# A Hymba-style layer on one core: GLA norm weights moved into W_out's rows, half a column group of FF1 weights loaded early, squares written elsewhere

## The chip, the cores and the metric

The kernel runs on one core of a Trainium2 chip (trn2). The metric is the device time of one execution in microseconds (us). Engines are named as the profile names them: PE (TensorE, matmuls; PEld is its weight load), DVE (VectorE), ACT (ScalarE), POOL (GpSimd) and SP (SyncE, which issues most DMAs). L12 is line 12 of the kernel before.

## The reference

One decoder layer with two parallel mixers, on 2048 tokens of width 1024, all in float32. The part that the change touches, shortened:

```python
nx = rmsnorm(h, attn_norm_g)
proj = einsum('bsd,dp->bsp', nx, w_in)
gq, gk, gv, gr, glow, dq, dk_, dv_ = split(proj)
o_a = gla_mixer(gq, gk, gv, glog)                       # 4 heads, gated linear attention
o_a = o_a * lax.rsqrt(mean(o_a * o_a, axis=-1) + EPS)
o_a = o_a * gla_norm_g.reshape(GLA_HEADS, GLA_DV)        # 512 norm weights
o_a = o_a.reshape(B, S, 512) * silu(gr)
o_b = dilated_mixer(dq, dk_, dv_, rel_bias)              # 8 heads, three windows
h = h + concat([o_a, o_b]) @ w_out
y = rmsnorm(h, mlp_norm_g)
h = h + square(relu(y @ w_ff1)) @ w_ff2                  # 1024 -> 4096 -> 1024
out = rmsnorm(h, final_norm_g)
```

The norm weights multiply the 512 columns of the first mixer, whose product with W_out's first 512 rows follows, so they can stand at three places: in the gate values silu(gr), in o_a, or in W_out's rows.

## The kernel before, in words

**Number format.** Each float32 operand is split in two, a rounded high part (ACT, `AF.Copy`) and the rest (DVE, source minus high part): `split`, L489 to L491. A product is three matmuls, high by high, rest by high, high by rest (L140 to L142). The large products are done blockwise with 7 instead of 8 block products ("jobs" j = 1 to 7), whose operands are sums of blocks.

**Stages**, one behind the other with some overlap: the input projections (to about 520 us, in two passes of 1024 tokens each), attention of both mixers (to about 870 us), W_out with the second norm (850 to 1045 us), FF1 (to 1750 us) and FF2. In the projections the order of each engine is the program's; behind them a scheduler sets each engine's order from its own estimate of times, and buffers are slots of a common pool, so a load starts when the last reader of its slot is done.

**Gate values.** For the column group "gr" the projection's result goes through silu in `acc` (L353 ACT exponential, L354 DVE product), L355 multiplies it on POOL by the norm weights, held in all partitions as `gnB` in the tile `misc`, and SP stores it to `srD`. The same stage keeps DVE busy with weight sums and splits (`wcomb`, L288 to L300) and with the blocks' sums (`acc`, L342, L442 to L458). SP's queue is in order, so its weight loads (`wraw`) and the stores of q (`qD`) stand in line with these stores.

**W_out.** `load_wo` (L1115) loads 8 row chunks of 128; the chunks c < 4 belong to the first mixer and are split into the blocks (1, c) and (12, c), the others are kept whole. `sum_wo` (L1130) loads chunks c and c + 4 together, forms four differences on POOL and stores them to `wtD`, from where `mix_wo` (L1143) loads and splits them later. All of this runs within attention's time.

**The second norm.** `norm_row` (L1289) takes one row block of 128 tokens: the squares with their sum on ACT (L1292, written to `scr`, which nobody reads), the scaling on DVE (L1294), eight transposes on PE, two copies on ACT into the block's half of `bb` (L1300, quarters `hb4`), and stores to `hTD`. `norm_sums` (L1303) forms four sums of a pair of blocks on DVE (L1307 to L1310) and stores them too. `bb` holds one pair; `gs` holds the norm weights of the second norm in its first half, and `scr` is its second half.

**FF1.** 16 column groups of 256 (g), each in two halves k of four row chunks. `load_w1` (L1381) brings a half by a POOL DMA into one of two raw tiles `w1raw`, `prep1` (L1389) splits and sums for a job. W_out's loop calls the first loads: group 0 at its step 49, group 1 at step 54, and prepares FF1's jobs from step 54. The first jobs are mixed of both groups: (0,1), (0,2), (0,6), (1,1), (0,5), (1,2), and so on, pairs of group and job; (1,1) needs half 0 of group 1, (1,2) needs half 1.

## Time and profile before

| | |
|---|---|
| three runs | 2235.83, 2241.91, 2242.97 us; median 2241.91 us |
| the profiled execution | 2242.91 us, its span 2241.1 us, mean granted clock 0.997 |
| POOL's multiplies L355 | 32, in 79 to 131 us and in 329 to 381 us |
| POOL's loads of FF1's raw weights L1387 | 64 of 512 KB, from 1025.4 to 1617.0 us |
| ACT's squares L1292 | 16, from 879.2 to 1063.5 us |

How to read the profile: a line of groups gives the source line, engine, operation, output tile <- input tiles, shape, count, then busy time and mean duration of one, and the idle time of the engine ahead of them with what ended it. A line of waits gives who waited for whom, the total in us, how often, and the longest. A line of the timeline gives start, duration, engine, line, operation; in brackets the idle time before it and its releaser. A line of windows gives the stretch, then for each engine busy time and count, then TensorE's granted clock (1.00 is full), the DMA engines' share and GB/s. Instructions overlap a little in the timeline, so the chain of waits shows the same ones somewhat shorter.

### The profile page before, as it was taken

How to read it: one execution, taken by the hardware profiler on the slowest of the kernel's cores; microseconds unless marked ns; L12 is line 12 of the kernel's file. 1: busy time of each engine (PE TensorE's matmuls, PEld its weight loads, DVE VectorE, ACT ScalarE, POOL GpSimd, SP SyncE). 2: the span in 40 equal slices, each digit the busy share in tenths (PEclk: the TensorE clock that was granted, in tenths of full speed). 3: DMA queues.
4: the chain of work that ended last, by engine and by line, in shares of the span. 5: the costliest groups of instructions: out<-in, count | busy, mean ns of one | idle time of the engine just before them, and what ended most of it. 6: DMA issues, size and time to landing. Idle time of an engine off the chain costs nothing.

```text
span 2241.1 us, 35330 instructions
## 1 busy us (share of the span) xinstructions
PE 2212.8 (99%) x12420; PEld 1918.8 (86%) x12420; DVE 1680.8 (75%) x3173; ACT 1253.5 (56%) x2506; POOL 533.6 (24%) x535
## 2 busy tenths in 40 slices
PE   9999999999999999999999999999999999999998
PEld 8978998799999998887888888888888888888877
DVE  8787868666677677778777788777685697576798
ACT  7675446435787785555655566555555433333446
POOL 1110001016577673000000000000006222031462
PEclk9999999999999999999999999999999999999999
DMA  6467854787977877767744456555489988677775
GB/s 214 141 188 229 256 165 121 213 250 251 312 256 222 271 214 241 247 225 249 220 141 149 140 177 199 165 167 167 130 279 287 306 282 276 216 250 253 250 258 197
DMA packets 340934, 491.79 MB, mean 219 GB/s; under 512 B 20503, under 2 KB 237162, under 8 KB 330004
## 3 DMA queue, kind: packets, MB, share of 16 engines
q1 hardware_dynamic: 319842, 394.88, 54.6%
q0 software_dynamic: 13568, 41.95, 7.6%
q10 hardware_dynamic: 7346, 52.70, 6.3%
q8 instruction: 98, 1.61, 0.3%
q14 instruction: 80, 0.66, 0.1%
HBM read 335.52 MB, written 158.66 MB: 221 GB/s over the span
## 4 chain that ended last, share of the span: by engine, by line
PE 68%; issue 16%; DVE 7%; DMA 5%; POOL 2%; ACT 1%; SPq 0%; POOLq 0%; ACTq 0%; DVEq 0%
PE ps_a L141 7%; PE ps_a L142 6%; PE ps_a L140 6%; PE ps_c L141 5%; PE ps_c L142 5%; PE ps_c L140 5%; PE ps_a L909 4%; PE ps_d L141 3%; PE ps_d L142 3%; PE ps_d L140 3%; PE ps_o L141 3%; PE ps_o L140 3%; PE ps_o L142 3%; PE ps_d L890 3%; PE ps_c L872 2%
## 5 line engine op out<-in xcount | busy, mean ns | idle before, releaser
L490 ACT ACTIVATE cb<-bs 128x1024 fp32r<-128x1024 f32 x104 | 110.1, 1059 | 287.9 <-PE ps_o L141 94.6
L491 DVE TENSOR_TENSOR cb<-bs,cb 128x1024 fp32r<-128x1024 f32 x104 | 157.9, 1519 | 137.7 <-ACT cb L490 137.4
L1680 POOL TENSOR_TENSOR bs<-bs,rb 128x1024 f32<-128x1024 f32 x60 | 174.3, 2912 | 318.1 <-DMA bs<-w_ff 282.4
L491 DVE TENSOR_TENSOR w1comb<-w1raw,w1comb 128x512 fp32r<-128x512 f32 x224 | 153.2, 686 | 94.0 <-ACT w1comb L490 93.9
L1387 POOL DMA_DIRECT2D w1raw<-w_ff x64 | 48.2, 754 | 702.6 <-DVE w1comb L491 532.8
L490 ACT ACTIVATE w1comb<-w1raw 128x512 fp32r<-128x512 f32 x224 | 139.9, 627 | 92.0 <-PE ps_c L142 27.2
L881 ACT ACTIVATE pe<-pe,O 128x256 f32<-128x256 f32 (+1 forms) x384 | 157.5, 454 | 45.6 <-DVE O L880 41.9
L909 PE MATMUL ps_a<-v,pt 128*128 128x65 f32 x1200 | 180.8, 253 | 1.5 <-DVE pt L899 1.4
L909 PEld LDWEIGHTS ps_a<-v,pt 128*128 128x128 f32 x1200 | 175.7, 195 | 2.9 <-DVE pt L899 1.7
L880 DVE CUSTOM_DVE_ANT_0 pe<-ps_c,nb 128x256 f32<-128x256 f32 (+1 forms) x384 | 126.7, 360 | 46.8 <-PE ps_d L890 16.5
L890 PE MATMUL ps_d<-ident,pe 128*128 128x128 f32 x600 | 160.5, 281 | 0.0
L288 ACT ACTIVATE wcomb<-wraw 128x512 fp32r<-128x512 f32 (+2 forms) x119 | 90.1, 757 | 99.2 <-PE ps_a L141 33.0
L140 PE MATMUL ps_c<-hb,w1comb 128*128 128x512 f32 x320 | 124.6, 390 | 0.0
L141 PE MATMUL ps_c<-hb,w1comb 128*128 128x512 f32 x320 | 124.4, 389 | 0.0
L142 PE MATMUL ps_c<-hb,w1comb 128*128 128x512 f32 x320 | 124.1, 389 | 0.0
L491 DVE TENSOR_TENSOR ca<-ra,ca 128x1024 fp32r<-128x1024 f32 x84 | 121.8, 1451 | 0.1
L141 PE MATMUL ps_c<-cb,ca 128*128 128x512 f32 x312 | 121.5, 389 | 0.0
L140 PE MATMUL ps_c<-cb,ca 128*128 128x512 f32 x312 | 121.5, 389 | 0.0
L142 PE MATMUL ps_c<-cb,ca 128*128 128x512 f32 x312 | 121.4, 389 | 0.0
L890 PEld LDWEIGHTS ps_d<-ident,pe 128*128 128x128 f32 x600 | 109.2, 186 | 0.3
L355 POOL TENSOR_TENSOR acc<-acc,misc 128x264 f32<-128x264 f32 (+1 forms) x32 | 29.4, 924 | 319.3 <-DVE acc L354 303.9
L140 PE MATMUL ps_a<-wcomb,tb 128*128 128x256 f32 (+1 forms) x344 | 97.7, 284 | 0.0
(476 smaller groups left out, 7248.8 us busy)
## 6 DMA issues: line engine op xcount, KB each, us to landing
ra<-actD ACTq DMA_DIRECT2D x50, 1024.0 KB, 7.3
actD<-ring SPq DMA_DIRECT2D x176, 256.0 KB, 3.1
rb<-w_ff SPq DMA_DIRECT2D x88, 512.0 KB, 5.3
bs<-w_ff SPq DMA_DIRECT2D x72, 512.0 KB, 6.0
w1raw<-w_ff POOLq DMA_DIRECT2D x64, 512.0 KB, 5.3
k<-kD SPq DMA_DIRECT2D x16, 1024.0 KB, 7.9
rb<-hTD SPq DMA_DIRECT2D x28, 512.0 KB, 5.8
wraw<-w_in SPq DMA_DIRECT2D x48, 256.0 KB, 3.6
```

The lines of the kernel that those rows point to most:

```text
L140: T.matmul(out, sh, mh, start=first, stop=False, **kw)
L141: T.matmul(out, sl, mh, start=False, stop=False, **kw)
L142: T.matmul(out, sh, ml, start=False, stop=last, **kw)
L288: A.activation(hi, src, AF.Copy, scale=sc)
L490: A.activation(hi, src, AF.Copy)
L491: V.tensor_tensor(lo, src, hi.bitcast(F32), op=OP.subtract)
L880: V.tensor_tensor_reduce(p, s, bias, scale=1.0, scalar=BIG, op0=OP.add, op1=OP.min, accum_out=nm)
L881: A.activation(p, p, AF.Exp, bias=nm, scale=-1.0)
L890: T.transpose(pb[:, i * 128:i * 128 + 128], src, ident)
L909: T.matmul(self.b.opsum[:, n % 4], self.pt[:, i * 128:i * 128 + 128], self.b.v[:, blk, cols], start=first, stop=last)
L1387: G.dma_start(raw1[g % 2][:, 4 * k:4 * k + 4], w1[:, 4 * k:4 * k + 4, g0:g0 + 256])
L1680: (engines or ((G,), (V, V))[len(sums) - 1])[e].tensor_tensor(v, v, r, op=OP.add if op == "+" else OP.subtract)
```

## The change

Three edits. **First**, the norm weights are no longer multiplied on POOL. A DMA puts them in four columns of the tile `stats` (128 partitions x 4), and W_out's first 512 rows are scaled by them: in `load_wo` both halves of a split take the scale (ACT by its scale operand, DVE by a scalar_tensor_tensor), in `sum_wo` one added ACT copy scales 128x1024 in place. The broadcast into `misc` is shorter by 512 columns, and the ring of small statistics has 44 in place of 48 columns. **Second**, half 0 of FF1's group 1 is loaded at W_out's step 50 into the second half of `gs`, not into a slot of `w1raw`; half 1 follows at step 54 as before. **Third**, the squares of a row block go to that block's own half of `bb`, which the two copies of L1300 fill afterwards; so a square has to wait until the previous pair's stores to `hTD` and sums (L1310) have read `bb`.

```diff
--- before.py
+++ after.py
@@ -159,10 +159,11 @@
     V.memset(eps, EPS)
     V.memset(mhalf, -0.5)
     stats = const.tile([128, 48], F32, name="stats")
+    gn = stats[:, 44:]
     stat_at = [0]
 
     def stat(n=1):
-        if stat_at[0] + n > 48:
+        if stat_at[0] + n > 44:
             stat_at[0] = 0
         s = stats[:, stat_at[0]:stat_at[0] + n]
         stat_at[0] += n
@@ -231,7 +232,7 @@
 
 
     misc = slot("misc", FR)
-    gB, gnB = misc[:, :D].bitcast(F32), misc[:, D:D + 512].bitcast(F32)
+    gB = misc[:, :D].bitcast(F32)
     w2b, w2raw = misc[:, D + 512:D + 768], misc[:50, D + 768:D + 1024]
     gTs = [misc[:, D + 768 + 128 * i:D + 896 + 128 * i] for i in range(2)]
     small = const.tile([128, 96], F32, name="small")
@@ -261,7 +262,7 @@
     TB = {j: [view(t, (4, 512)) for t in TF[j]] for j in order}
     xs = [t[:, D * q:D * q + D] for t in (xp, bp) for q in range(2)] + [c22[:, :D], last[:, :D]]
     xs += [xt[:, D * q:D * q + D] for q in range(2)]
-    gD, wD = dram.tile([1, D + 512], F32, name="gD"), dram.tile([17, 256], F32, name="wD")
+    gD, wD = dram.tile([1, D], F32, name="gD"), dram.tile([17, 256], F32, name="wD")
     nTD = dram.tile([7, 128, 4, 512], F32, name="nTD")
 
     def load_w(g, n, k):
@@ -352,7 +353,6 @@
             log_sigmoid(sg, s[:, :m])
             A.activation(sg, sg, AF.Exp)
             V.tensor_tensor(s[:, :m], sg, s[:, :m], op=OP.mult)
-            G.tensor_tensor(s[:, :m], s[:, :m], gnB[:, j:j + m], op=OP.mult)
             SP.dma_start(srD[tk, j:j + m], s[:, :m])
             if m < w:
                 gate(s[:, m:w], t)
@@ -682,10 +682,10 @@
             for k in range(2):
                 load_w(1, n, k)
         SP.dma_start(gD[:, :D], a["attn_norm_g"])
-        SP.dma_start(gD[:, D:], a["gla_norm_g"])
+        SP.dma_start(gn, a["gla_norm_g"].rearrange("o (c p) -> p (o c)", p=128))
         SP.dma_start(wD[:16], a["gla_gate_w2"].rearrange("o r k -> (o r) k"))
         SP.dma_start(wD[16:], a["gla_gate_b"])
-        SP.dma_start(misc[:, :D + 512].bitcast(F32), bcast_row(gD, D + 512))
+        SP.dma_start(gB, bcast_row(gD, D))
         for r, n in ((0, 17), (17, 16), (33, 17)):
             SP.dma_start(w2raw[r:r + n].bitcast(F32), wD[:n])
         pv = turned(4)
@@ -1120,7 +1120,10 @@
             SP.dma_start(raw, wo[:, c])
             if c < 4:
                 for j, n in ((1, 0), (12, 1)):
-                    split(*block_view(j, c), raw[:, 512 * n:512 * n + 512])
+                    hi, lo = block_view(j, c)
+                    r = raw[:, 512 * n:512 * n + 512]
+                    A.activation(hi, r, AF.Copy, scale=gn[:, c:c + 1])
+                    V.scalar_tensor_tensor(lo, r, gn[:, c:c + 1], hi.bitcast(F32), op0=OP.mult, op1=OP.subtract)
             else:
                 w = WO[c - 4] = view(slot("wo", FR), (2, D))
                 split(w[:, 0], w[:, 1], raw)
@@ -1133,6 +1136,7 @@
         for k in range(2):
             SP.dma_start(raw[:, D * k:D * k + D], wo[:, c + 4 * k])
         yield
+        A.activation(raw[:, :D], raw[:, :D], AF.Copy, scale=gn[:, c:c + 1])
         b11, b12, b21, b22 = [raw[:, 512 * k:512 * k + 512] for k in range(4)]
         for dst, x, y in ((b12, b12, b11), (b22, b22, b12), (b21, b21, b22), (b11, b22, b11)):
             G.tensor_tensor(dst, x, y, op=OP.subtract)
@@ -1276,7 +1280,7 @@
 
 
     gs, bb = slot("gs"), slot("bb")
-    gM, scr = gs[:, :D], gs[:, D:2 * D]
+    gM, early = gs[:, :D], view(gs[:, D:2 * D], (4, 256))
     hb4 = [view(bb[:, 512 * q:], (4, 128)) for q in range(4)]
     rb, TF, TB = [], {}, {}
     norms = []
@@ -1289,10 +1293,10 @@
     def norm_row(h, t):
 
         ss = stat()
-        A.activation(scr, h, AF.Square, accum_out=ss)
+        k = t % HT // 4
+        A.activation(bb[:, D * k:D * k + D], h, AF.Square, accum_out=ss)
         r = rstd_of(ss, D)
         V.scalar_tensor_tensor(h, h, r, gM, op0=OP.mult, op1=OP.mult)
-        k = t % HT // 4
         for q in range(2):
             pv = view(ps("c"), (4, 128))
             for c in range(4):
@@ -1380,11 +1384,15 @@
 
     def load_w1(g, halves=(0, 1)):
         if g < 2 * NP:
-            if len(raw1) < 2:
-                raw1.append(view(slot("w1raw"), (CH, 256)))
             g0 = g % NP * 256
             for k in halves:
-                G.dma_start(raw1[g % 2][:, 4 * k:4 * k + 4], w1[:, 4 * k:4 * k + 4, g0:g0 + 256])
+                if (g, k) == (1, 0):
+                    to = early
+                else:
+                    if len(raw1) <= g % 2:
+                        raw1.append(view(slot("w1raw"), (CH, 256)))
+                    to = raw1[g % 2][:, 4 * k:4 * k + 4]
+                G.dma_start(to, w1[:, 4 * k:4 * k + 4, g0:g0 + 256])
 
     def prep1(at):
 
@@ -1394,8 +1402,8 @@
         if not combs1:
             combs1.extend(view(c[:, 1024 * q:], (2, 4, 128)) for c in [slot("w1comb", FR) for _ in range(2)]
                           for q in range(2))
-        r = raw1[g % 2]
-        (a11, a12), (a21, a22) = [[r[:, 4 * k:4 * k + 4, n * 128:n * 128 + 128] for k in range(2)] for n in range(2)]
+        r = [early if g == 1 else raw1[g % 2][:, :4], raw1[g % 2][:, 4:]]
+        (a11, a12), (a21, a22) = [[r[k][:, :, n * 128:n * 128 + 128] for k in range(2)] for n in range(2)]
         c = combs1[at % 4]
         split(c[:, 0], c[:, 1], {1: a11, 2: a12, 6: a11, 5: a21, 7: a11, 3: a12, 4: a22}[j])
         if j == 2:
@@ -1604,8 +1612,10 @@
             raw_block(p + 1, 1, 1)
             load_mix(p + 2)
         half0(g - 56)
+        if g == 50:
+            load_w1(1, (0,))
         if g in (49, 54):
-            load_w1(int(g > 49))
+            load_w1(*((0, (0, 1)) if g == 49 else (1, (1,))))
         if g >= 54:
             prep1(g - 54)
 
```

What stands on the engines at the places in question. POOL in the projections, before (tile names as in the text; `stats` belongs to the start, `qp` to attention):

```order
11 L503 TENSOR_TENSOR stats<-stats,pair 128x1 x8
12 L355 TENSOR_TENSOR acc<-acc,misc 128x264 x8
13 L355 TENSOR_TENSOR acc<-acc,misc 128x248 x8
14 L355 TENSOR_TENSOR acc<-acc,misc 128x264 x8
15 L355 TENSOR_TENSOR acc<-acc,misc 128x248 x8
16 L823 COPY qp<-qs 128x512 x4
17 L777 MEMSET v 128x16x2
```

With the change POOL goes from row 11 straight to the copies of `qp`; PE's, ACT's and DVE's order in the projections stays the same.

DVE near the end of attention, before (`wb` and `woraw` are W_out's split and raw rows, L880 the reductions of the scores, L1095 an update of the GLA state):

```order
1496 L491 TENSOR_TENSOR wb_9347<-woraw,wb_9347 128x512
1497 L491 TENSOR_TENSOR wb_9350<-woraw,wb_9350 128x512
1498 L880 ISA pe,O_9511<-ps_c,nb_5223 128x128
1499 L880 ISA O_9511 128x1
1500 L880 ISA pe,O_9511<-ps_c,nb_5223 128x256
1501 L880 ISA O_9511 128x1
1502 L880 ISA pe,O_9511<-ps_c,nb_5223 128x256
1503 L880 ISA O_9511 128x1
1504 L1095 TENSOR_TENSOR gla<-gla,ps_o 64x256 x2
```

And now (lines of the changed kernel; L1126 is the scaled split):

```order
1495 L1126 TENSOR_SCALAR wb_9319<-woraw,stats,wb_9319 128x512
1496 L1126 TENSOR_SCALAR wb_9322<-woraw,stats,wb_9322 128x512
1497 L1095 TENSOR_TENSOR gla<-gla,ps_o 64x256 x2
1498 L880 ISA pe,O_9483<-ps_c,nb_5191 128x128
1499 L880 ISA O_9483 128x1
```

The update of the GLA state has moved from behind the three reductions to ahead of them.

ACT at the start of FF1, before (`hb` and `rb` are split and raw activations, `xs` a saved product, `ps_a` and `ps_c` PE's results):

```order
1071 L490 ACTIVATE hb_11559<-rb 128x1024
1072 L490 ACTIVATE w1comb<-w1raw 128x512 x3
1073 L1300 ACTIVATE bb<-ps_c 128x512 x2
1074 L1292 ACTIVATE gs,stats<-xh 128x1024
1075 L173 ACTIVATE stats<-stats,pair 128x1
1076 L174 ACTIVATE stats<-stats 128x1
1077 L490 ACTIVATE w1comb<-w1raw 128x512
1078 L1470 ACTIVATE xs_11596<-ps_a 128x512
```

And now:

```order
1078 L490 ACTIVATE hb_11532<-rb 128x1024 x2
1079 L175 ACTIVATE stats<-stats 128x1
1080 L490 ACTIVATE w1comb<-w1raw 128x512 x2
1081 L490 ACTIVATE w1comb<-gs 128x512
1082 L1304 ACTIVATE bb<-ps_c 128x512 x2
1083 L490 ACTIVATE w1comb<-w1raw 128x512 x2
1084 L1478 ACTIVATE xs_11568<-ps_a 128x512
1085 L490 ACTIVATE hb_11584<-rb 128x1024 x2
1086 L490 ACTIVATE w1comb<-w1raw 128x512
```

The third split of FF1 weights reads `gs` in place of `w1raw`, and the square that stood between the copies to `bb` and the next split has moved behind the rows shown. On POOL the early load stands between L965 (the weighting of a head group's branches) and L967 (their sum); the other 63 loads stand where the 64 stood.

## The prediction

> **What bounds the kernel now.** I read the page first, then TensorE's waits, then the granted clock around the longest of them, and last the rows of each wait. The profiled execution took 2242.91 us (span 2241.1 us plus 1.8 us around it).
>
> ```profile
> PE 2212.8 (99%) x12420; PEld 1918.8 (86%) x12420; DVE 1680.8 (75%) x3173; ACT 1253.5 (56%) x2506; POOL 533.6 (24%) x535
> ...
> L355 POOL TENSOR_TENSOR acc<-acc,misc 128x264 f32<-128x264 f32 (+1 forms) x32 | 29.4, 924 | 319.3 <-DVE acc L354 303.9
> ```
>
> TensorE is the bound and the change leaves its matmuls as they are. Only its idle time and the time at a lower clock can be won: 2241.1 - 2212.8 = 28.3 us and a little more. The 29.4 us of multiplies that GpSimd loses are no gain in themselves.
>
> ```profile
> PE ps_d L140 <- ACT w1comb L490: 3.5, 3, 2.5
> ...
> PE ps_a L140 <- ACT acc L445: 2.0, 1, 2.0
> PE ps_c L1299 <- DVE xh L1294: 1.8, 2, 1.1
> PE ps_c L870 <- DVE O L880: 1.6, 1, 1.6
> PE ps_a L909 <- DVE pt L899: 1.4, 1, 1.4
> ```
>
> These are the largest waits that can be reached; each has its place below. Two of them are followed by stretches at half clock (busy time of PE, PEld, DVE, ACT, POOL, then the granted clock):
>
> ```profile
> 397.10:400.50 3.40, 1.38 (x7) 0.95 (x6) 0.30 (x1) 0.93 (x2) 0.00 (x0) 1.00 0.80 164
> 400.50:403.90 3.40, 3.40 (x10) 2.49 (x10) 2.85 (x5) 2.44 (x7) 0.00 (x0) 0.50 0.47 139
> ...
> 823.80:830.60 6.80, 5.41 (x30) 5.11 (x29) 6.22 (x20) 6.35 (x18) 6.65 (x7) 0.50 0.49 156
> 1043.00:1047.50 4.50, 2.02 (x14) 1.50 (x13) 2.83 (x6) 0.69 (x2) 0.00 (x0) 1.00 1.00 370
> ```
>
> 3.4 us at half clock cost 1.7 us of work, 6.8 us cost 3.4 us. The wait of 1047 us had no such sequel.
>
> **Part 1: the multiplies of L355 go, first pass of the projections.** Nobody on TensorE waits for L355. What it does is slow VectorE beside it. VectorE's rows with a multiply running, then two rows with GpSimd empty:
>
> ```profile
> 115.05 1.07 DVE L442 TENSOR_TENSOR acc<-ps_a,acc 128x512 f32<-128x512 f32 x1
> ...
> 128.26 1.22 DVE L290 TENSOR_TENSOR wcomb<-wraw,wcomb 128x512 fp32r<-128x512 f32 x1
> ...
> 129.73 1.05 DVE L455 TENSOR_TENSOR acc<-ps_o,acc 128x512 f32<-128x512 f32 x1
> ...
> 135.52 0.67 DVE L442 TENSOR_TENSOR acc<-ps_c,acc 128x512 f32<-128x512 f32 x1
> 136.12 0.67 DVE L290 TENSOR_TENSOR wcomb<-wraw,wcomb 128x512 fp32r<-128x512 f32 x1
> ```
> ```profile
> 115.20 0.73 POOL L355 TENSOR_TENSOR acc<-acc,misc 128x248 f32<-128x248 f32 x1 [3.15 <-DVE acc L354]
> ```
>
> From 115 to 131 us five 128x512 instructions are stretched like this while VectorE has no slack: two by 0.40 (the first one here and one of L447), one of L342 by 0.35, L290 by 1.22 - 0.67 = 0.55, L455 by 0.38, together **2.1 us**. VectorE's backlog reaches TensorE only behind them:
>
> ```profile
> 136.85 0.50 PE L141 MATMUL ps_o<-tb,wcomb 128*128 128x512 f32 x1 [0.69 <-DVE wcomb L290]
> ...
> 157.70 0.28 PE L318 MATMUL ps_d<-misc 128*128 128x256 f32 x1
> 158.31 0.50 PE L140 MATMUL ps_a<-tb,wcomb 128*128 128x512 f32 x1 [0.34 <-ACT wcomb L288]
> ...
> 160.24 0.39 PE L142 MATMUL ps_a<-tb,wcomb 128*128 128x512 f32 x1
> ```
>
> A 128x512 matmul starts every 0.23 us, so 157.70 to 160.24 (2.54 us) holds 0.11 + 3 x 0.23 = 0.80 us of work: 1.7 us are lost, and at 136.85 another 0.69 plus the refill, 0.8. Of these 2.5 us the 2.1 us of VectorE can lift 2.1. Ends: 1.0 us (if half of VectorE's gain is lost in its waits for loads) and 2.5 us (all). I take **-2.1 us**.
>
> The Trainium skill (SBUF — State Buffer, "Who interferes with whom") says that a VectorE instruction with at most one SBUF input does not contend with GpSimd, one with two does. L442 and L455 here read one input from PSUM and are stretched all the same, by 0.40 and 0.38 us, so the measurement decides against it. By that rule only L342 and L290 (0.9 us a pass) would shrink, and the sum would be about 2.4 us higher.
>
> **Part 1, second pass.** The same five are stretched again (first and last of them), and behind them comes the longest wait of the stage:
>
> ```profile
> 363.93 1.07 DVE L442 TENSOR_TENSOR acc<-ps_a,acc 128x512 f32<-128x512 f32 x1
> ...
> 380.29 1.05 DVE L455 TENSOR_TENSOR acc<-ps_c,acc 128x512 f32<-128x512 f32 x1
> ```
> ```profile
> 371.90 5.55 DMA wraw<-w_in
> ...
> 391.79 7.70 DMA qD<-acc
> 399.57 0.61 ACT acc L445
> 400.22 0.56 PE ps_a L140
> ```
>
> In the chain of waits a store of 7.70 us, issued when VectorE gets there, lets ScalarE copy and TensorE go on. With the store issued 2.1 us earlier the wait of 2.0 us nearly goes; TensorE arrives earlier too, by about 0.8 us of smaller waits before it, so some 0.8 us are left. Whatever is left is shorter than the idle time (2.0 of 3.4 us) ahead of the half clock at 400.5 us, which I expect to go with it: 2.1 + 1.7 = **-3.8 us**. Ends: -1.0 us, if the store's 7.70 us are the queue's and it lands when it did, and -4.5 us.
>
> The Trainium skill (TensorE: Matmul & The Clock Gate, Part 1, "What's actually happening") puts the lower clock behind at least one idle window of about 3.4 us. The row of 397.10 has 1.38 us of work in such a window, so less than a whole idle window was enough here. By the page's rule the half clock at 400.5 us would not hang on a wait of 2.0 us and could stay: 1.7 us more; that is part of rival 1.
>
> **Part 1, what is added.** Four scale copies of 128x1024 on ScalarE (1.05 us each, as the square of that size in part 3) and eight scaled splits in place of plain ones, equal in size. In the attention stage ScalarE idles for VectorE (the page's row for its exponentials), so 4.2 us over some 50 us hide; each would cost about 1 us if it stood ahead of a score unit's copy. I take +0.3 us of 0 to +4.
>
> ```profile
> L881 ACT ACTIVATE pe<-pe,O 128x256 f32<-128x256 f32 (+1 forms) x384 | 157.5, 454 | 45.6 <-DVE O L880 41.9
> ```
>
> In VectorE's order at the end of attention the two-part addition of L1095 comes before three score reductions where it came behind:
>
> ```profile
> 817.88 3.47 DVE L491 TENSOR_TENSOR wb<-woraw,wb 128x512 fp32r<-128x512 f32 x2 [0.93 <-ACT wb L490]
> ...
> 822.29 0.84 DVE L1095 TENSOR_TENSOR gla<-gla,ps_o 64x256 f32<-64x256 f32 x2
> ```
>
> The two splits (3.47 us beside GpSimd's work) already hold back those reductions, for which TensorE waits 1.6 us. The addition makes it **+0.8 us**, and the half clock behind stays. Ends: +2.5 (the half clock one window longer) and -6 (rival 2).
>
> **Part 2: the early half.** Before, the loads go out when TensorE frees the slot, and the third split waits for them:
>
> ```profile
> 1038.54 1.50 POOL L1387 DMA_DIRECT2D w1raw<-w_ff  x2 [11.35 <-PE ps_a L142]
> ```
> ```profile
> 1039.31 1.14 ACT L490 ACTIVATE w1comb<-w1raw 128x512 fp32r<-128x512 f32 x2
> 1046.81 0.63 ACT L490 ACTIVATE w1comb<-w1raw 128x512 fp32r<-128x512 f32 x1 [6.37 <-DMA w1raw<-w_ff]
> ...
> 1049.92 0.61 ACT L490 ACTIVATE w1comb<-w1raw 128x512 fp32r<-128x512 f32 x1
> ```
> ```profile
> 1044.54 0.48 PE L140 MATMUL ps_c<-hb,w1comb 128*128 128x512 f32 x1
> 1047.49 0.50 PE L140 MATMUL ps_d<-hb,w1comb 128*128 128x512 f32 x1 [2.48 <-ACT w1comb L490]
> ```
>
> 2.95 us instead of 0.23 between two matmuls: 2.7 us lost. With the half loaded some 180 us ahead the split follows the first two at about 1040.5 us, 6 us sooner; next late is the other half, which goes out at the same 1038.5 us, now alone, while the splits behind this one ran from 1049.9 us on. **-2.7 us**, ends -1.5 and -3.3.
>
> The early load itself is one more issue on GpSimd (0.75 us, row below) between L965 and L967, ahead of the mix that W_out's rows wait for, and 512 KB in a busy stretch of the DMA engines. TensorE waits only 0.5 us there (at 869 us). I take **+0.7 us**, ends 0 and +2.
>
> ```profile
> PE ps_a L140 <- DVE O L912: 0.5, 1, 0.5
> ```
> ```profile
> L1387 POOL DMA_DIRECT2D w1raw<-w_ff x64 | 48.2, 754 | 702.6 <-DVE w1comb L491 532.8
> ```
>
> **Part 3: squares into the rows' own buffer.** They now wait until the pair's last readers are done, VectorE's L1310 and the stores. Before, for one pair:
>
> ```profile
> 898.93 1.05 ACT L1292 ACTIVATE gs<-xh 128x1024 f32<-128x1024 f32 x1
> ```
> ```profile
> 902.40 0.68 DVE L1310 TENSOR_TENSOR xh<-xh,bb 128x512 f32<-128x512 f32 x1
> ```
>
> At the old place this square would wait 903.1 - 898.9 = 4.2 us, and ScalarE's copies and splits queued behind it too. In the new order the squares stand behind those copies and splits, so little is behind them. **+0.3 us**, ends 0 and +10 (rival 3). The load of the norm weights in small pieces takes the place of a small load in the same queue, and the page names no wait of TensorE for that queue after the start; I allow **+0.2 us** of 0 to +1.
>
> **Sum:** -2.1 - 3.8 + 0.3 + 0.8 - 2.7 + 0.7 + 0.3 + 0.2 = -6.3 us, so 2242.9 - 6.3 = 2236.6 us from this execution; from the median of the runs (2241.91) it would be 2235.6. I say **2236.0 us**.
>
> **Rivals.**
> 1. The projections don't gain: the loads and the 7.70 us store set the pace, TensorE only waits later, the half clock stays. Only about 1 us of the two passes is left instead of 5.9: 2241 us. For it: 5.55 us and 7.70 us of the chain are DMA. Against it: those loads are issued when VectorE or GpSimd frees a buffer. Chance 0.2.
> 2. The bunching at 818 us falls apart because everything before it is shifted: 1.6 + 1.4 + 3.4 us of half clock go and the 0.8 isn't paid: 2229 to 2232 us. Against it: the same two splits stand ahead of the same reductions. Chance 0.15.
> 3. Slower: ScalarE stands at the squares. From the pair above, 4.2 us for each of 7 pairs; TensorE has about one product's 12 matmuls in hand (12 x 0.23 = 2.7 us), so it decides as soon as a wait passes 2.7 us: 7 x 1.5 = 10.5 us, giving 2247 us. For it: ScalarE works in order. Against it: the new order. Chance 0.12.
> 4. The wait at 1047 us only changes its name (rows of hT or the other half land late): 2239 us. Chance 0.05.
>
> **How the numbers follow.** Forecast 0.48 (2233.5 to 2239). What this kernel's measurement can tell from no change is about 0.3%, here 6.7 us: faster below 2235.2, slower above 2248.6. Faster: half of the forecast's spread (0.24) and rival 2: 0.39. Slower: half of rival 3, 0.06. Same: 0.55. The range 2230 to 2244 leaves out rival 3 and the lower part of rival 2.
>
> **What would show it.** In the changed profile 128x512 instructions of VectorE near 115 and 364 us at 0.67; no waits of TensorE at 136, 158 to 160 and 400 us, clock 1.00 at 400 to 404; no wait for w1comb at FF1's start; a longer wait near 820 us; no wait at ScalarE's squares longer than 2 us that TensorE follows. It is wrong if TensorE's sum of waits below 410 us stays, or if new waits in W_out for ScalarE's copies appear.

## The result, and the profile after

| | before | changed |
|---|---|---|
| median (lowest to highest), 17 runs each | 2240.14 (2235.83 to 2246.28) us | 2245.65 (2239.28 to 2257.58) us |
| profiled execution, its span | 2242.91, 2241.1 us | 2241.9, 2240.0 us |

The ratio is 1.0027, 95% interval 1.0016 to 1.0038: the changed kernel is a little slower, by less than the 0.3% that the prediction called distinguishable, and its median lies above the predicted range (2230 to 2244). Two later sets of runs of the same kernel gave 1.0006 (0.9991 to 1.0020) and 1.0013 (1.0002 to 1.0025). So by these intervals it lies between 0.1% faster and 0.4% slower, where 0.3% faster was forecast, and its runs spread over 18 us where those of before spread over 10. The profiled execution is the second quickest of its 17, while that of before lies in the upper half of its own, so comparing these two traces shows less than the 5.5 us between the medians.

First the page of the changed kernel: TensorE's work is the same, GpSimd has lost 25 us and ScalarE gained 6, and the span is where it was.

```profile
PE 2212.3 (99%) x12420; PEld 1918.0 (86%) x12420; DVE 1673.9 (75%) x3173; ACT 1259.7 (56%) x2510; POOL 508.5 (23%) x503
```

TensorE's waits in it (who <- whom: total, times, longest). Between L162 and L354 the changed kernel's lines are one higher than before, from there to L1115 the same, and behind that 3 to 10 higher.

```profile
PE ps_a L140 <- ACT acc L445: 1.8, 1, 1.8
PE ps_a L140 <- DVE O L912: 1.8, 1, 1.8
PE ps_o L1034 <- issue: 1.6, 1, 1.6
...
PE ps_a L140 <- ACT w1comb L490: 1.0, 1, 1.0
```

The wait for w1comb of 2.5 us has become one of 1.0 us at another place; the wait of 400 us (L445) is 1.8 instead of 2.0 us; the 0.5 us for O L912 at W_out's start have become 1.8 us; the 1.6 us at 820 us stand under another name (L1034, which starts when the update L1095 ends). The windows that the prediction quoted, now:

```profile
397.10:400.50 3.40, 3.03 (x9) 2.29 (x10) 2.61 (x5) 2.89 (x8) 0.00 (x0) 0.64 0.57 153
400.50:403.90 3.40, 3.40 (x15) 2.75 (x14) 2.95 (x8) 0.83 (x2) 0.00 (x0) 0.86 0.44 164
...
1043.00:1047.50 4.50, 4.50 (x26) 3.86 (x25) 4.13 (x7) 1.88 (x4) 0.00 (x0) 1.00 0.99 347
```

The half clock behind the wait of 397 us is still there (0.64 and 0.86 are one stretch of 3.41 us at 0.50 that lies across both windows). At 1047 us TensorE now works through.

**Where the time went.** All kernels here have the same 12420 matmuls, so the start of the n-th matmul can be compared with that of before. Behind 520 us the scheduler can put another matmul at the n-th place, which moves a value inside a stage by up to about 1 us (eight transposes); at a stage's ends that is even again. The table gives how much each stretch (in before's time, us) became longer (+) or shorter (-) against the profiled execution of before; a row adds up to the whole difference at 2230 us. The three rows of the changed kernel are three of its executions, and the last row is the forecast's own steps.

| | to 100 | 100-300 | 300-520 | 520-800 | 800-850 | 850-1044 | 1044-1050 | 1050-1200 | 1200-2230 | sum |
|---|---|---|---|---|---|---|---|---|---|---|
| changed | +0.4 | -2.1 | -0.8 | +0.6 | -0.7 | +1.6 | -2.9 | +4.0 | -1.2 | -1.1 |
| again | -0.7 | -1.7 | -1.1 | +0.3 | -0.7 | +2.0 | -2.9 | +4.3 | -0.5 | -0.8 |
| third | -0.5 | -1.3 | -1.9 | **+5.5** | +0.1 | +2.7 | -2.9 | +4.0 | -1.3 | +4.5 |
| forecast | 0 | -2.1 | **-3.8** | +0.3 | +0.8 | +1.0 | -2.7 | **0** | 0 | -6.5 |

(The forecast's +0.2 for the load of the norm weights had no place and is left out.) Three terms carry the miss: the second pass (-0.8 to -1.9 instead of -3.8), the attention stage in some executions (up to +5.5 instead of +0.3), and FF1 behind the wait that went (+4.0 to +4.3, where the sum has nothing).

### The profile page after: what moved, and what is told of

Same layout as the page of the kernel before. It is cut to its first block, busy times and chain, and to the rows that moved or that the text cites. A ratio compares the mean times of both kernels' runs of the same rounds, so it can differ in the third digit from the quotient of the medians.

```text
span 2240.0 us, 35237 instructions
## 1 busy us (share of the span) xinstructions
PE 2212.3 (99%) x12420; PEld 1918.0 (86%) x12420; DVE 1673.9 (75%) x3173; ACT 1259.7 (56%) x2510; POOL 508.5 (23%) x503
## 4 chain that ended last, share of the span: by engine, by line
PE 83%; issue 6%; DMA 4%; DVE 4%; ACT 2%; POOL 1%; SPq 0%; POOLq 0%; ACTq 0%; DVEq 0%
PE ps_a L141 8%; PE ps_a L142 8%; PE ps_a L140 8%; PE ps_c L141 7%; PE ps_c L142 7%; PE ps_c L140 7%; PE ps_a L909 4%; PE ps_d L141 4%; PE ps_d L142 4%; PE ps_d L140 4%; PE ps_o L141 4%; PE ps_o L142 4%; PE ps_o L140 4%; PE ps_d L890 3%; PE ps_c L872 2%
## 5 line engine op out<-in xcount | busy, mean ns | idle before, releaser
L823 POOL CAST qp<-qs 128x512 fp32r<-128x512 f32 x64 | 68.7, 1153 | 461.8 <-PE ps_a L141 450.7
L880 DVE CUSTOM_DVE_ANT_0 pe<-ps_c,nb 128x256 f32<-128x256 f32 (+1 forms) x384 | 125.8, 360 | 46.6 <-PE ps_d L890 13.6
L491 DVE TENSOR_TENSOR ca<-ra,ca 128x1024 fp32r<-128x1024 f32 x84 | 115.3, 1373 | 0.1
```

Of the source, the lines that this page charges most:

```text
L491: V.tensor_tensor(lo, src, hi.bitcast(F32), op=OP.subtract)
L823: G.tensor_copy(dst, src)
L880: V.tensor_tensor_reduce(p, s, bias, scale=1.0, scalar=BIG, op0=OP.add, op1=OP.min, accum_out=nm)
```

## The experiments

Unless a diff says otherwise, a kernel is the one before plus the lines shown. A row of a table by stages is one execution: that of `after_no_min` is the quickest of its 12, that of `fold_dve` the longest of its 12. Each expectation names its own theories; those that matter for the whole are: in attention, **U** (the added ScalarE work itself costs) against **V** (the work hides, but the engines' new order, and VectorE's small instructions held up by GpSimd, cost), and for FF1 whether the squares, the sums or the order of the splits takes the 4 us.

### Each edit alone, and the changed kernel once more

`norm_only` is the first edit alone (the norm weights), `squares_only` the third:

```diff
-        A.activation(scr, h, AF.Square, accum_out=ss)
+        k = t % HT // 4
+        A.activation(bb[:, D * k:D * k + D], h, AF.Square, accum_out=ss)
```

`early_squares` is the second and third edit together, since the early half needs the place that the squares leave:

```diff
+        if g == 50:
+            load_w1(1, (0,))
         if g in (49, 54):
-            load_w1(int(g > 49))
+            load_w1(*((0, (0, 1)) if g == 49 else (1, (1,))))
```

`after_again` is the changed kernel as it is.

> The kernel before with the first edit alone (norm weights in W_out's rows). Theory A, the loss of the whole change is made at W_out's end and FF1's start by the other two edits: this one keeps the 2.5 us that the projections gained in the profile and loses up to 1 us in attention, so 1 to 3 us faster than before. Theory B, the loss comes from this edit, which gives attention and W_out another order: 3 to 7 us slower than before, with the time lost between 520 and 1045 us.

> The kernel before with the third edit alone (squares into the rows' own buffer); only W_out's order changes. Theory A: 1 to 3 us slower, lost between 880 and 1070 us, since ScalarE's squares wait for the last readers of that buffer. Theory B: within 1 us of before.

> The kernel before with the second and third edits (early half of group 1 and squares in the rows' buffer), norm weights still multiplied on GpSimd. Theory A: 5 to 8 us slower than before: the wait of 2.7 us at 1047 us goes, but waits between 1050 and 1120 us and in W_out cost more. Theory B: 0 to 3 us faster, since the wait at 1047 us goes and nothing else changes.

> The changed kernel once more, for its spread and a second profile. Both theories: 4 to 7 us slower than before in the median. If the spread of its runs (2239 to 2258 us) comes from the clock, the mean granted clock of its slow runs is lower than that of the fast ones; if it comes from waits, the clock is the same and this profile has waits at other places than the first.

| | median (range), us | ratio to before (95%) |
|---|---|---|
| norm_only | 2243.67 (2236.68 to 2249.24) | 1.0003 (0.9989 to 1.0016) |
| squares_only | 2245.71 (2240.68 to 2254.50) | 1.0013 (0.9999 to 1.0026) |
| early_squares | 2240.79 (2237.28 to 2244.93) | 0.9992 (0.9979 to 1.0004) |
| after_again | 2242.96 (2239.39 to 2254.01) | 1.0006 (0.9991 to 1.0020) |

| | to 100 | 100-300 | 300-520 | 520-800 | 800-850 | 850-1044 | 1044-1050 | 1050-1200 | 1200-2230 |
|---|---|---|---|---|---|---|---|---|---|
| norm_only | -0.5 | -1.5 | -0.9 | +5.8 | +0.1 | -1.3 | +0.3 | +0.2 | +0.5 |
| squares_only | -0.1 | +0.3 | +0.4 | 0.0 | -1.3 | -2.1 | +2.9 | +4.9 | +1.9 |
| early_squares | +1.1 | +1.0 | -0.2 | +1.1 | +0.8 | -3.1 | -2.9 | +4.0 | -1.1 |

None of the edits is a clear gain or loss by itself. The first wins 2.4 us in the projections and gives it back in attention; the second and third win 2.9 us at 1047 us and lose 4.0 behind it. Where the projections were left alone (the two lower rows) they still moved by 0.7 to 0.8 us in sum, and by up to 1.3 us in one column (`nosq_before` below: +1.1 and -1.3), which is how far such a table can be read. `norm_only` lost its time where theory B had it, but its median does not show 3 us; for `squares_only` 1 to 3 us were expected, and 2.9 came without being clear of noise, in FF1 rather than in W_out; `early_squares` fits its theory B.

`after_again` asked whether the spread comes from the clock. In part it does. Of the first 17 runs the two with a mean granted clock of 0.993 took 2251.84 and 2257.58 us, the seven with 0.998 took 2239.28 to 2250.13 us; of the 12 of `after_again` the two with 0.995 took 2252.81 and 2254.01 us, the seven with 0.998 took 2239.39 to 2243.93 us. A clock lower by 0.003 is 6.7 us of work in 2240 us, which is four stretches of 3.41 us at half clock; the three traced executions have one to three of them ahead of the kernel's end. No run above 2247.46 us of the changed kernel was traced, so where the longest ones lose their time stays open.

The 5.8 us of `norm_only` lie at one place. Its GpSimd and VectorE there (start, duration, instruction; idle time before it in brackets):

```profile
702.52 2.10 POOL L823 CAST qp<-qs 128x512 fp32r<-128x512 f32 x2
704.59 1.27 POOL L967 TENSOR_TENSOR O<-O,cmb 128x512 f32<-128x512 f32 x1
705.81 2.04 POOL L823 CAST qp<-qs 128x512 fp32r<-128x512 f32 x2
707.81 1.27 POOL L967 TENSOR_TENSOR O<-O,cmb 128x512 f32<-128x512 f32 x1
```
```profile
704.16 4.95 DVE L944 TENSOR_TENSOR gla<-O,cmb 128x16 f32<-128x16 f32 x1
709.15 0.17 DVE L945 TENSOR_TENSOR gla<-gla,cmb 128x16 f32<-128x16 f32 x1
```

A minimum of 128x16 elements, whose sister behind it takes 0.17 us, occupies VectorE for 4.95 us and ends when GpSimd's row of instructions ends. The scores' reductions stand behind it, and TensorE waits for them (its wait and the windows around it):

```profile
710.10 0.38 PE L870 MATMUL ps_c<-k,qs 128*128 128x256 f32 x1 [3.15 <-DVE O L880]
```
```profile
706.50:710.00 3.50, 0.45 (x4) 0.24 (x3) 3.47 (x7) 0.27 (x1) 3.16 (x6) 1.00 0.43 146
710.00:713.40 3.40, 3.30 (x18) 3.30 (x19) 2.53 (x12) 3.37 (x10) 1.77 (x4) 0.56 0.00 0
```

3.2 us of waiting and the half clock behind it, 1.7 us, are most of the 5.8. In the profiled execution of the changed kernel the same instruction, in the same order, passed, and in its third execution it did not:

```profile
704.29 0.49 DVE L944 TENSOR_TENSOR gla<-O,cmb 128x16 f32<-128x16 f32 x1
704.81 1.21 DVE L945 TENSOR_TENSOR gla<-gla,cmb 128x16 f32<-128x16 f32 x1
```
```profile
702.95 4.93 DVE L944 TENSOR_TENSOR gla<-O,cmb 128x16 f32<-128x16 f32 x1
```

That is the +5.5 of the third row of the table above. No difference in arrival is seen that would decide it: L944 starts 1.64 us behind the start of the two casts in `norm_only` and 1.67 us behind it in the third execution, where it was held, 1.65 and 1.66 us behind it in the first and in `after_again`, where it passed. Where it passed, it ended 0.04 us behind the casts, and L945 0.03 us behind the L967 that follows; where it was held, it ended 0.03 to 0.04 us behind the last L967. Either way VectorE's instruction ends where one of GpSimd's ends, and the traces don't show what lets it in at the one boundary or the other.

### The multiplies alone

`no_mul` leaves the norm weights out (no multiply, nothing in its place); attention and W_out keep their order. `no_mul_early` adds the second and third edit.

```diff
-            G.tensor_tensor(s[:, :m], s[:, :m], gnB[:, j:j + m], op=OP.mult)
```

> The kernel before with GpSimd's multiply by the norm weights left out and nothing put in its place; all else is as before. Theory P (the prediction): the two projection passes end 5.9 us earlier (2.1 + 3.8), since every stretched instruction of VectorE shrinks. Theory Q: only instructions with two SBUF inputs shrink; those that add a PSUM result to a strided tile (L442, L447, L450, L455 near 114 and 362 us) stay at 1.06 us with GpSimd idle, because of their stride, so the passes end 2 to 3.5 us earlier and a wait of 1 to 2 us of TensorE for ScalarE's L445 near 397 us stays, behind a store of q of 7 us or more.

> The second and third edits on the kernel without the multiply (norm weights left out). If the early half is worth its 2.7 us, 6 to 7 us faster than before. If FF1's start gives it back (theory T), as fast as without the multiply alone, 3 to 5 us faster than before, with the wait at FF1's first splits gone and about 4 us of waits between 1050 and 1120 us.

`no_mul`: 2236.40 us (2234.18 to 2244.71), ratio 0.9984 (0.9971 to 0.9997). `no_mul_early`: 2235.68 us (2232.79 to 2239.77), 0.9975 (0.9965 to 0.9985).

| | to 100 | 100-300 | 300-520 | 520-800 | 800-850 | 850-1044 | 1044-1050 | 1050-1200 | 1200-2230 |
|---|---|---|---|---|---|---|---|---|---|
| no_mul | -0.1 | -1.7 | -2.6 | 0.0 | -2.1 | -0.9 | +0.2 | 0.0 | +3.5 |
| no_mul_early | -0.8 | -2.4 | -2.5 | 0.0 | -0.3 | -2.2 | -2.9 | +4.6 | -0.9 |

So in these two executions the multiplies are worth 4.2 to 4.9 us in the projections, between theory P's 5.9 us and theory Q's 2 to 3.5, and by the medians of `no_mul` 0.16% of the whole time (0.03 to 0.29), as long as nothing takes their place in attention, which then runs from 520 to 800 us to the hundredth of a microsecond as before. (The +3.5 of `no_mul` behind 1200 us are mostly two waits of 2.4 and 1.2 us at 2150 us and a half clock there.) The changed kernel has only 2.8 to 3.2 of these; but the other kernels without the multiplies, whose projections are the same, have 1.2 (`sums_on_pool`) to 4.1 us (`after_no_min`), so that is spread, and no cause of its own is shown for it. What VectorE's instructions in the projections do without any multiply beside them, in the changed kernel:

```profile
113.92 1.05 DVE L442 TENSOR_TENSOR acc<-ps_a,acc 128x512 f32<-128x512 f32 x1
...
116.62 0.67 DVE L343 TENSOR_TENSOR acc<-acc 128x512 f32<-128x512 f32 x1
...
125.36 0.69 DVE L291 TENSOR_TENSOR wcomb<-wraw,wcomb 128x512 fp32r<-128x512 f32 x1
...
127.96 1.07 DVE L455 TENSOR_TENSOR acc<-ps_o,acc 128x512 f32<-128x512 f32 x1
```

L343 and L291 (L342 and L290 before) have become short, as forecast. They are two of eight: from 80 to 129 us these and six more that the forecast did not price (one each of L208, L571, L354, L577, L292 and L458 of before) are shorter than before by 0.2 to 0.6 us each, together 3.8 us, and all eight have two inputs and neither of them from PSUM. L571, before and in the changed kernel:

```profile
97.54 1.25 DVE L571 TENSOR_TENSOR bp<-bp 128x512 f32<-128x512 f32 x1
```
```profile
98.01 0.69 DVE L571 TENSOR_TENSOR bp<-bp 128x512 f32<-128x512 f32 x1
```

L442 and L455 are as long as ever, though the forecast took 0.40 and 0.38 us off each. In the kernel before, in a stretch with no multiply at all, they were long too:

```profile
158.24 1.02 DVE L442 TENSOR_TENSOR acc<-ps_a,acc 128x512 f32<-128x512 f32 x1
...
172.20 1.03 DVE L455 TENSOR_TENSOR acc<-ps_c,acc 128x512 f32<-128x512 f32 x1
```

The trace's records of their operands differ where the profile has the same 128x512: the long ones read and write their SBUF tile as 8 x 16 x 4 elements, the L442 of 0.67 us that the forecast compared them with reads 512 in one piece. The ones of 8 x 16 x 4 take 1.02 to 1.10 us in the traces of before, of the changed kernel and of `no_mul` there, with and without a multiply.

### Is it the copies, and where they run?

`norm_no_copy` is the first edit without the four added ScalarE copies (so 512 rows of W_out lack the norm weights in the blockwise products), `scale_on_pool` has them on GpSimd, and `fold_dve` adds no instruction: two of the four differences go to VectorE with the scale folded in, the later splits take the rest.

```diff
-        A.activation(raw[:, :D], raw[:, :D], AF.Copy, scale=gn[:, c:c + 1])
```
```diff
-        A.activation(raw[:, :D], raw[:, :D], AF.Copy, scale=gn[:, c:c + 1])
+        G.tensor_scalar(raw[:, :D], raw[:, :D], gn[:, c:c + 1], None, op0=OP.mult)
```
```diff
-        A.activation(raw[:, :D], raw[:, :D], AF.Copy, scale=gn[:, c:c + 1])
...
+        G.tensor_tensor(b12, b12, b11, op=OP.subtract)
+        V.scalar_tensor_tensor(b22, b12, g, b22, op0=OP.mult, op1=OP.subtract)
+        G.tensor_tensor(b21, b21, b22, op=OP.add)
+        V.scalar_tensor_tensor(b11, b11, g, b22, op0=OP.mult, op1=OP.add)
```

> The first edit alone, without its four added copies on ScalarE (four of W_out's chunks stay unscaled in the mixed products). Theory U (the added ScalarE work is what the first edit costs behind the projections): as fast as without the multiply, 3 to 5 us faster than before. Theory V (another order of attention costs by itself, because VectorE's two-input operations stand behind whatever GpSimd runs just then): 2 us faster to 2 us slower than before, with VectorE instructions of 128x8 or 128x16 of over 2 us in the trace and a wait of TensorE behind them.

> The first edit alone, the four added copies on GpSimd in place of ScalarE (about 2 us each). Theory U: 2 to 4 us faster than before, since ScalarE is free of them. Theory V: within 2 us of the first edit with ScalarE copies, up or down, since GpSimd's work only lands at other moments.

> The first edit without added instructions: the scale is folded into two of the four differences of each W_out chunk (they go from GpSimd to VectorE, where an operation with a scale exists) and into the scales of the later splits; norm weights are in, squares and FF1 as before. Theory U: 3 to 5 us faster than before, as without the multiply, since nothing is added to ScalarE and GpSimd has less to do. Theory V: the gain of the projections (4 us) stays if GpSimd's order near 703 us does not hold VectorE, else 0 to 2 us slower than before.

| | median (range), us | ratio (95%) | 100-520 | 520-800 | 800-1044 |
|---|---|---|---|---|---|
| norm_no_copy | 2238.57 (2236.38 to 2244.71) | 0.9990 (0.9979 to 1.0001) | -3.8 | 0.0 | -3.1 |
| scale_on_pool | 2242.61 (2239.50 to 2251.58) | 1.0006 (0.9994 to 1.0018) | -3.1 | +2.6 | -0.1 |
| fold_dve | 2241.93 (2235.99 to 2246.97) | 0.9998 (0.9988 to 1.0009) | -1.7 | +3.7 | +2.4 |

Without the copies attention is untouched and L944 took 1.10 us; by its median (0.10% faster) `norm_no_copy` lies between the theories, and V's sign, a small VectorE instruction of over 2 us, isn't there, so this run alone fits U. Against U stand two others: the changed kernel has the copies and lost only 0.6 and 0.3 us in two of its executions, and `scale_on_pool` lost 2.6 us without any added ScalarE work. So ScalarE's added 4.2 us are neither enough for the loss nor needed for it. That the hold of L944 makes the loss is shown for `norm_only` and the third execution alone: `scale_on_pool` (L944 0.46 us) and `fold_dve` (0.68 us) lose without it. Both put work on other engines, so they don't part added work from a new order. TensorE's waits in `fold_dve`, 520 to 870 us:

```profile
PE ps_a L909 <- ACT pt L897: 3.3, 2, 2.7
PE ps_c L1386 <- DMA mx<-mixD: 1.8, 1, 1.8
PE ps_a L909 <- DVE pt L899: 1.4, 1, 1.4
```

### The two minima taken away

In `after_no_min` (the changed kernel) and `before_no_min` the minima L944 and L945 are left out for three of the four head groups, the first branch's value standing in their place.

```diff
-        tc.keep_in_program_order(V.tensor_tensor(M, nm[0], nm[1], op=OP.min))
-        V.tensor_tensor(M, M, nm[2], op=OP.min)
+        if pr < 3:
+            M = nm[0]
```

> The changed kernel without the two small VectorE minima of each combine step (L944 and L945 of before; the first branch's value stands in for the minimum of the three, for the first three head pairs), which were held for 4.9 us by GpSimd in two of the traces. Theory V (the hold near 703 us, which a difference of 0.1 us in the arrival decides, makes the slow executions and so the loss in the median): no wait of TensorE over 1.5 us between 560 and 800 us, 2 to 4 us faster than the changed kernel in the median and a spread of under 10 us. Theory W (the loss is made elsewhere, at attention's end and in W_out): within 1 us of the changed kernel.

> The kernel before without the same minima, as control: within 1 us of before (both theories), since its trace shows no hold between 560 and 800 us.

> The changed kernel a third time, on the same chip as these three: 1 to 5 us slower than before in the median. Its projections end 2.5 to 3.5 us earlier than before in the trace; what was gained is gone by 1120 us.

`after_no_min`: 2242.19 us (2237.45 to 2246.32), ratio 1.0000 (0.9989 to 1.0011); attention 0.0 from 520 to 800, no hold in the one trace, the spread 9 us instead of 14 to 18, and no run with a mean granted clock under 0.997. That fits the hold as a cause of the changed kernel's long executions; it does not show it, as the control tells. `before_no_min`, where nothing was to be won and both theories expected no change, became slower: 2248.24 us (2237.38 to 2253.73), 1.0028 (1.0013 to 1.0043), +4.9 us from 520 to 800, with waits that before has not there:

```profile
PE ps_a L909 <- ACT pt L897: 3.4, 2, 1.9
PE ps_c L870 <- DVE O L880: 3.0, 1, 3.0
```

So removing instructions as small as 0.17 us, two in each of three head groups, went with a loss of 5 us. The minima can't be taken out without the scheduler putting the rest in another order, and the order weighs more than they do. `after_third`: 2244.53 us (2237.69 to 2251.96), 1.0013 (1.0002 to 1.0025).

### FF1's start

In the changed kernel 4.0 to 4.3 us are lost between 1050 and 1200 us, beyond what before loses there at two waits of 0.5 us. TensorE's waits from 1040 to 1125 us in the changed kernel, and in `squares_only`:

```profile
PE ps_a L140 <- ACT w1comb L490: 1.0, 1, 1.0
PE ps_c L140 <- ACT xs L1478: 0.7, 1, 0.7
PE ps_c L140 <- ACT w1comb L490: 0.5, 1, 0.5
PE ps_c L141 <- DVE w1comb L491: 0.2, 1, 0.2
PE ps_o L141 <- DVE w1comb L491: 0.2, 1, 0.2
```
```profile
PE ps_d L140 <- ACT w1comb L490: 4.9, 2, 3.8
PE ps_c L140 <- DVE acc L1476: 1.9, 1, 1.9
PE ps_a L140 <- ACT w1comb L490: 0.5, 1, 0.5
```

The largest in the changed kernel, of 1058.30 us, on TensorE and on ScalarE:

```profile
1058.30 1.01 PE L140 MATMUL ps_a<-hb,w1comb 128*128 128x512 f32 x2 [0.98 <-ACT w1comb L490]
```
```profile
1057.13 0.60 ACT L1478 ACTIVATE xs<-ps_a 128x512 f32<-128x512 f32 x1 [0.83 <-PE ps_a L142]
1057.63 0.62 ACT L490 ACTIVATE w1comb<-w1raw 128x512 fp32r<-128x512 f32 x1
1058.80 1.06 ACT L1297 ACTIVATE bb<-xh 128x1024 f32<-128x1024 f32 x1 [0.55 <-DVE xh L1554]
```

The split that TensorE needs stands behind the copy of a product that TensorE has yet to end, and ScalarE idles 0.83 us for it: TensorE ends, waits for copy and split, goes on. The square of 1058.80 us stands behind both and is not what is waited for here. The kernel before has the same row of copy and split, with 3.37 us of idle time ahead of it, and TensorE does not wait for that split, because eight transposes of the second norm stand there and last until it is done:

```profile
1060.52 0.60 ACT L1470 ACTIVATE xs<-ps_a 128x512 f32<-128x512 f32 x1 [3.37 <-PE ps_a L142]
1061.01 0.62 ACT L490 ACTIVATE w1comb<-w1raw 128x512 fp32r<-128x512 f32 x1
```
```profile
1060.78 1.03 PE L1299 MATMUL ps_c<-ident,xh 128*128 128x128 f32 x8
```

In the changed kernel the eight transposes run at 1064.17 us, where nothing is waited for. So at this place it is not the split's place on ScalarE alone, but that TensorE's order no longer covers it. The other small waits have other makings: at 1086.48 us, for one, the split came late because ScalarE idled 3.15 us for a load of FF1 weights.

Three kernels asked who is to blame. `nosq_before` and `nosq_early` leave the squares out (a constant in place of their sum), the second one with the early half; `sums_on_pool` is the changed kernel with the pair's sums on GpSimd.

```diff
-        A.activation(scr, h, AF.Square, accum_out=ss)
+        V.memset(ss, float(D))
```
```diff
-        V.tensor_tensor(b12, b12, b11, op=OP.subtract)
+        G.tensor_tensor(b12, b12, b11, op=OP.subtract)
```

(and so for the other three sums.)

> The kernel before without the 16 squares (the sum of squares is a constant; the second norm is left out). It is the control for the next one. TensorE's wait for w1comb at the start of FF1 stays at 2.5 to 4 us (both theories), since it is the load that is late.

> The kernel before with the early half of group 1 and without the 16 squares. Theory S (the squares' later place on ScalarE gives the gain of the early half back): the wait near 1047 us is gone and the waits from 1050 to 1120 us sum to under 2 us instead of 4.1, so FF1's start gains over 2 us against its control. Theory T (preparing FF1's first groups is the bound there, on VectorE and ScalarE, whatever the squares do): the waits from 1050 to 1120 us sum to 3 to 5 us, and nothing is gained between 1044 and 1120 us.

> The changed kernel with the four sums of each pair of rows (L1307 to L1310 of before) on GpSimd in place of VectorE, which has 35 us of work in the 40 us behind 1040 us. Theory T: the waits from 1050 to 1120 us fall from 4.1 to under 2.5 us, and the kernel is 1 to 3 us faster than the changed one. Theory S: they stay at 4 us or grow, since GpSimd's sums take longer and the squares wait for them.

| | time, us | ratio (95%) | 850-1044 | 1044-1050 | 1050-1200 |
|---|---|---|---|---|---|
| nosq_before | 2248.61, one run | | -2.4 | +2.1 | +3.4 |
| nosq_early | 2246.34, one run | | -2.9 | -2.2 | +7.8 |
| sums_on_pool | 2254.85 (2253.45 to 2267.83) | 1.0084 (1.0052 to 1.0117) | +11.2 | -0.4 | +3.6 |

`nosq_before` kept its wait for w1comb at 1047 us (2.4 us). In `nosq_early`, taking the squares out altogether made this stretch longer, not shorter, through one wait elsewhere, behind which the clock stays at 0.50 for 6.83 us (3.4 us of work):

```profile
PE ps_c L1299 <- DVE xh L1294: 4.4, 1, 4.4
```

And with the sums on GpSimd VectorE's splits of W_out are late (TensorE, 1000 to 1125 us), while 3.6 us are lost behind 1050 us as well; theory T's gain did not come:

```profile
PE ps_a L141 <- DVE mcomb L491: 6.3, 3, 3.9
```

So neither the squares' time on ScalarE nor the sums' time on VectorE explains the 4 us. What is shown: every kernel with the early half loses 3.4 to 4.9 us there (7.8 without squares), and with the old loads and squares the first edit's four variants of this study lose 0.1 to 0.5. The changed kernel's three executions, `after_no_min`, `early_squares` and `no_mul_early` lose it at the same five places (near 1061, 1079, 1091, 1099 and 1119 us of before's time); the others with the early half lose it at other ones, `nosq_early` in the one wait above and `scale_rows_early` mostly behind a half clock at 1108.7 us. And `squares_only` and `nosq_before` lose 4.9 and 3.4 without an early half, each with a half clock among it (1115.0 and 1048.7 us). So several new orders of the engines there cost about as much. Which part of the new order is at fault stays open but for the largest wait.

### The weights applied outside attention

If the loss belongs to attention's order, the weights should be applied where attention has ended. `scale_rows` and `scale_rows_early` (this one with the second and third edit) put them on W_out's other operand, the transposed rows, where these are copied from PSUM. They compute all that the reference does.

```diff
-            A.activation(raw0[0][:, 2 * e + q], mix_block(p, e, q, "c"), AF.Copy)
+            pv, to = mix_block(p, e, q, "c"), raw0[0][:, 2 * e + q]
+            if q == 0:
+                V.tensor_tensor(to, pv, gn.unsqueeze(2).to_broadcast([128, 4, 128]), op=OP.mult)
+            else:
+                A.activation(to, pv, AF.Copy)
```

> The multiplies of L355 are left out as in the change, but the norm weights now go on the rows instead of on W_out's weights: in W_out's loop the transposed rows of the first mixer get them where they are copied from PSUM (12 copies move from ScalarE to VectorE as products, 4 splits become four scaled pieces each). Attention has no added and no exchanged instruction, W_out's own stage has. Theory V (the change loses in attention what it wins in the projections, because the scaled weights give attention's engines another order): the start of the same matmul stays 4 to 5 us earlier than before from 520 to 818 us with nothing lost in between, and the time is 2 to 4 us below before's unless W_out's loop pays for it on VectorE. Theory U (applying the weights costs wherever it is done, since it is work): 2 to 4 us are lost between 870 and 1045 us and the time is within 1 us of before's.

> The same, with the early half and the moved squares of the change (edits 2 and 3). It computes all that the reference does. Theory V: as the kernel with edits 2 and 3 and no norm weights at all (0.9975 of before's time): 2234 to 2238 us. Theory U: 2239 to 2243 us, as edits 2 and 3 alone. In both the waits of FF1's start (1047 us) are as in the changed kernel: the wait of 2.7 us gone, about 4 us in small waits from 1050 to 1120 us.

| | median (range), us | ratio (95%) | 100-520 | 520-800 | 800-850 | 850-1044 | 1044-1050 | 1050-1200 |
|---|---|---|---|---|---|---|---|---|
| scale_rows | 2241.63 (2239.44 to 2246.69) | 1.0005 (0.9995 to 1.0015) | -2.7 | 0.0 | -0.8 | +0.9 | -2.2 | +2.7 |
| scale_rows_early | 2244.44 (2240.43 to 2252.54) | 1.0017 (1.0005 to 1.0028) | -3.7 | +0.3 | -1.5 | +2.4 | -2.2 | +4.9 |

From 520 to 800 us attention is untouched, as V has it, though what the projections won is 2.7 and 3.7 us and not V's 4 to 5. But neither is faster: the time goes at the next places, W_out and FF1's start, in `scale_rows` without any edit of FF1. There one late sum and the half clock behind it take what was won:

```profile
1104.93 0.49 PE L140 MATMUL ps_d<-hb,w1comb 128*128 128x512 f32 x1 [0.49 <-ACT w1comb L490]
1107.02 0.59 PE L140 MATMUL ps_c<-hb,w1comb 128*128 128x512 f32 x1 [1.60 <-DVE acc L1476]
1107.41 0.63 PE L141 MATMUL ps_c<-hb,w1comb 128*128 128x512 f32 x1
```

V's time (2234 to 2238 us) did not come either, so it is not attention alone that answers to a new order. No kernel that computes everything was shown to beat the one before; `early_squares`, 0.9992 (0.9979 to 1.0004), comes nearest.

## Why the prediction was wrong, step by step

1. **First pass, -2.1: size right in part by luck, rows wrong.** Measured -1.3 to -2.1. Of the five instructions that the step priced, only L342 and L290 were stretched by GpSimd (0.9 us); L447's and L442's 0.40 and L455's 0.38 us, more than half of the term, are there without GpSimd too. What makes up for it are six stretched instructions ahead of 112 us, 2.9 us, which the step did not look at. The Trainium skill (SBUF — State Buffer, "Who interferes with whom") says that an instruction of VectorE with at most one SBUF input, outside its 2-port modes, does not contend with GpSimd. The prediction set two rows against that; the trace after agrees with the rule (1.05 and 1.07 us with GpSimd idle), and the rows were misread.
2. **Second pass, -3.8: the term mis-sized, -0.8 to -1.9.** The step let the store of 7.70 us go out earlier and the wait and the half clock go with it. The store did go out earlier, by 2.9 us (388.88 instead of 391.79), and landed earlier, but TensorE came earlier as well, so the wait is 1.8 us (1.1 in the other two executions), not the 0.8 that the step left, and in this execution the half clock behind it remains:

```profile
388.88 7.85 DMA qD<-acc
...
396.82 0.61 ACT acc L445
...
397.47 0.50 PE ps_a L140
```

   In the other two executions, in `norm_only` and in `no_mul` the half clock was gone, as forecast; in `fold_dve` and `sums_on_pool`, with the same projections, it stayed. So the step failed by the wait that it let shrink to 0.8, and the half clock, which it took to go with the wait, goes in some executions and stays in others. Even without it the pass won 0.9 to 2.6 us and never 3.8. That is rival 1 in part: about half of the 5.9 us of both passes came.
3. **The copies hide, +0.3: failed in some executions.** They hide as work (+0.6 and +0.3 us in two executions), and the price that the step kept as its upper end, copies ahead of a score unit's, is not what cost. What it did not price is the order: the scheduler's new order lines up casts and additions of GpSimd without a gap beside a small VectorE one, which was held 4.93 us in the third execution, and then 5.5 us go. The ends of 0 to +4 were too narrow, and they were bounds on the wrong thing.
4. **L1095 at 818 us, +0.8.** Measured -0.7, -0.7 and +0.1 from 800 to 850 us. The half clock near there lasted 3.41 instead of 6.83 us in all three executions, where the step let it stay; within the ends given. The wait itself did not grow in the profiled execution (1.6 us): TensorE now waits for the update L1095 in place of the reductions.
5. **W_out and the early load, +0.7 and +0.3 for the squares.** Measured +1.6 to +2.7 (the +2.7 with a half clock at 922 us). TensorE waits 1.8 us for O L912 at 868 us. The chain of that wait runs through L944, held 2.67 us at 852.75 us (0.90 before) by two GpSimd instructions that stand behind the early load's issue (0.98 us at 851.86), so the step looked at the right place. But the early load isn't shown to be the cause: `early_squares` and `no_mul_early` have it and are 2 to 3 us shorter in this stretch, and `norm_only` loses 1.2 us from 850 to 870 us without it.
6. **The early half, -2.7: the failed step that shows in every execution.** The wait went as forecast (-2.9), and "next late is the other half, which goes out at the same 1038.5 us, now alone" took it that nothing follows. 4 us follow. The step looked at the split that waited and not at what the engines do behind it: the term for 1050 to 1200 us was nothing, without a reason beyond the next load. ScalarE, VectorE and TensorE had the same work left in a new order, in which TensorE's transposes no longer cover a split that stands behind the copy of a product. Rival 4 (the wait changes its name, 0.05) comes nearest, but the late load that it named is seen at one of the small waits only, and its 2239 us left no loss beyond the gain.
7. **Rival 3**, ScalarE standing at the squares in W_out, was not seen: no wait of TensorE there names them.

Of the marks that the prediction gave for itself, these came as it said: no wait for w1comb at 1047 us, none at 136 us, none of TensorE at the squares, and a sum of TensorE's waits from 12 to 410 us that fell (4.2 us before, 2.6 now; 3.2 in the other two executions). Partly: the waits at 158 to 160 us fell from 0.9 to 0.3 us (0.6 in the other two), and the clock at 400 us is 1.00 in the other two executions only. The others didn't come: L442 and L455 stayed at 1.05 and 1.07, the wait of 400 us stayed, and the wait near 820 us did not grow.

## What to carry to other kernels

A wait that an edit takes away is worth only as much as the next stretch has slack: price the queue of every engine for some 50 us behind it, not the one instruction that waited. Where a scheduler decides the order, an edit inside a full stage brings a draw of a new order, here from 3 us won (W_out in `early_squares`) to 6 us lost (attention in `norm_only`), more than the edit's own work, so the range must hold that draw. Before a duration is called stretched, look for the same line in a stretch where its rival is idle.
